# A hybrid decoder layer on one core: the transfers of sample states, requested by GpSimd in place of SyncE

## The chip, the cores and the metric

The kernel runs on one core of a Trainium2 chip. The metric is the time of one execution on the device in microseconds, the median of several runs. One execution is also recorded by the hardware profiler; a time inside it is counted from the start of its span. The engines are called by their names or as the profile has them: TensorE (PE, and PEld for its weight loads), VectorE (DVE), ScalarE (ACT), GpSimd (POOL), SyncE (SP, which here only requests transfers). Each engine works through its own queue in order; a waiting instruction holds up what is queued behind it on that engine.

## The reference, cut to what matters

One layer of a decoder runs over 16 learned tokens and 256 prompt tokens, and over one new token for each of 8 sequences (the samples), which start from states kept in memory:

```python
x = layer_norm(ALPHA * x + 0.5 * swiglu(x, f1_g, f1_u, f1_d), ...)
m, s_ret, s_hg = token_mixer(x, ...)
x = layer_norm(ALPHA * x + m, ...)
x = layer_norm(ALPHA * x + 0.5 * swiglu(x, f2_g, f2_u, f2_d), ...)

def token_mixer(x, pos, s_ret, s_hg, ...):
    q_r, k_r, v_r, g_r, q_h, f_h, i_h, g_h, a_r, a_h = split(x @ w_in, 10)
    ...
    s_ret, o_r = retention_chunk(s_ret, q_r, k_r, v_r)       # 8 heads, state 256 x 256
    s_hg, o_h = hgrn2_chunk(s_hg, q_h, k_h, i_h, log(f))     # 16 heads, state 128 x 128
    ...
    y = sigmoid(a_r) * o_r + sigmoid(a_h) * o_h
    return y @ w_out, s_ret, s_hg
```

For a sample both chunk functions have length 1. The new state is a decay times the old one plus the outer product of key and value; the output is the query times the new state. The decay is a constant of the head (retention) or a value for each feature (HGRN2). All new states are outputs. D_MODEL is 2048, the feed-forward width 5504, all data float32.

## The kernel before, in words

Features lie on the 128 partitions, the 280 tokens (272 and 8 samples) on the free axis. Every weight matrix is cut into 128x128 blocks and streamed once, 8 blocks (512 KB) to a unit. `stream` (L170) loads a unit into `raw` (L185, SyncE), ScalarE rounds it to `whi` (L188), and VectorE takes the rest, `wlo = raw - whi` (L189). `dense` (L204) multiplies each block in three matmuls, `xh·whi`, `xl·whi` and `xh·wlo` (L218). `raw`, `whi` and `wlo` have three buffers each.

The work runs as first feed-forward (`up`, `dn`), mixer, output projection (`wo`), second feed-forward. In the mixer the projections (`pj_...`) are streamed in 8 rounds, one for each retention head `u`, with two HGRN2 heads in each. The branches' own work is written as generators, `mix_hg` and `mix_ret`, which are started when their inputs are there and advanced a piece after each row of blocks (`pump`, L617). So their matmuls and vector work lie between those of the projections. TensorE's order is that of the code. The order on the other engines is made by a scheduler from the code and its own model of times.

What a round moves for the samples, by line:

- `mix_ret`, `load(e)` (L1092, transfers in L1095): the retention states of four samples, two tiles `smr` of 512 KB for each half `e`. Half 0 is loaded a round ahead; half 1 when the buffers of `ks` and `vs` are free, after the state matmuls (L1168).
- `spread(i)` (L1153, L1156): two samples' value rows, written to memory by L730 (`vrd`) and read back to all 128 partitions as `vbr` (256 KB, two buffers). `spread(0)` and `spread(1)` come early, `spread(2)` and `spread(3)` when the updates with the first two are done.
- L1192 (ScalarE) scales the old state by the decay, held in `gam` (L1174, GpSimd) for half 0 and in `late` (named `sro` in the profile, L1186 and L1188, GpSimd) for half 1. L1198 (VectorE) adds key times value, 16 updates a round; half 1 uses spreads 2 and 3.
- L1202: the four new tiles go out (`out_srs`), and L1211 multiplies them with the queries.
- `mix_hg`: the same for two HGRN2 heads: `load(h)` (L770, `smh`), `values(h)` (L774, `vbh`), `samples(h)` (L998 and L999), and out in L1002 (`out_sgs`). A one-element copy by GpSimd (L769, L773) stands ahead of each load to order it behind earlier work.

GpSimd also gathers `ends` (L750, L751), `tails` (L1103, transposed by TensorE in L1116) and `meta` (L910, L990). All transfers but two are requested by SyncE, so those of the states stand in one queue with the weights' loads.

Of the kernel before, what the change touches and what calls it, by code (L numbers as in the profile page):

```python
# [18 lines left out]
P = 128  # L19
# [109 lines left out]
def trunk(ctx: ExitStack, tc: tile.TileContext, A, O):  # L129
    nc = tc.nc  # L130
# [416 lines left out]
    with tc.tile_pool(name="yp", bufs=1) as yp:  # L547
# [7 lines left out]
        with tc.tile_pool(name="mp", bufs=1) as mp:  # L555
# [7 lines left out]
            def tmp(name, shape=(P, T), bufs=1, dt=F32, tag=None):  # L563
                if name in rows:
                    rows[name] = rows[name][1:] + rows[name][:1]
                    return rp.tile(list(shape), dt, tag=rows[name][-1], name=name)
                return mp.tile(list(shape), dt, tag=tag or name, name=name, bufs=bufs)
# [80 lines left out]
            def evacuate(n, c0, c1, o0, o1, b0, b1):  # L648
# [33 lines left out]
                elif n == "v_r":  # L682
                    v = tmp("v", (P, 2, T))
                    nc.scalar.copy(v[:, 0, :], o0)
                    nc.scalar.copy(v[:, 1, :], o1)
                    start(mix_ret(c0 // 2, st["q_r"], st["k_r"], v), 24 if c0 == 2 else 3)
                elif n in ("g_r", "g_h"):
                    sg = tmp("gs", (P, TL), bufs=2)
                    t = tmp("gt", (P, TL), bufs=2)
                    nc.scalar.activation(sg, o0, AF.Sigmoid)  # L690
                    mul(t, sg, o0)
                    sa = tmp("gs", (P, TL), bufs=2)
                    nc.scalar.activation(sa, o1, AF.Sigmoid)
                    mul(t, t, sa)
                    u, e = divmod(c0, 2)
                    while u not in (done_r if n == "g_r" else done_h):
                        pump()
                    if n == "g_r":
                        y = tmp("y", (P, TL))
                        mul(y, t, on_r[u][:, e, :])  # L700
                        st["y"] = y
                    else:
                        y = st["y"]
                        nc.vector.scalar_tensor_tensor(
                            out=t, in0=t, scalar=ngt[:, c0 : c0 + 1], in1=on_h[u][:, e, :], op0=ALU.mult, op1=ALU.mult)

                        ys[c0] = y if c0 < EARLY else yp.tile([P, TL], F32, tag=f"y{c0}", name=f"y{c0}")
                        add(ys[c0], y, t)
                        if c0 < EARLY:
                            split(yh[c0], yl[c0], y)  # L710
# [16 lines left out]
            def rows_out(src, width, tag):  # L727

                scr = drp.tile([NS, width], F32, tag=tag + "d", name=tag + "d")
                nc.sync.dma_start(scr, src)  # L730
                return scr
# [14 lines left out]
            def mix_hg(u, f, k, q, v):  # L746
# [16 lines left out]
                sms, vbs = [], []  # L763

                def load(h):

                    sms.append(tmp("smh", (P, NS, P), bufs=2))
                    vbs.append(tmp("vbh", (P, NS, P), bufs=2))
                    nc.gpsimd.tensor_copy(sms[h][:, 0, :1], kts[0][:, 0, :1] if h else acc[:, 15:16])  # L769
                    nc.sync.dma_start(sms[h], A["sg"][2 * u + h])  # L770

                def values(h):
                    nc.gpsimd.tensor_copy(vbs[h][:, 0, :1], kts[1][:, 0, :1] if h else acc[:, 2 * P + 15 : 2 * P + 16])  # L773
                    nc.sync.dma_start(vbs[h], vrow[h].partition_broadcast(P))  # L774


                Ts = {1: f}
# [92 lines left out]
                vrow = []  # L870
# [85 lines left out]
                if split_up:  # L956
                    load(0)
                    yield 4
                else:
                    for h in range(2):  # L960
                        if u:
                            fill(first(h), 1, h)
                        fill(second(h), 4, h)
                        if h == 0:
                            load(0)
                        yield 4
                for s in (16, 32, 64):
                    keep(tops[s], s)
                values(0)
                yield 15 if u == 1 else 2  # L970
                Tt = Ts[2 * LEVELS[-1]]
# [22 lines left out]
                def samples(h):  # L994
                    vb, sm = vbs[h], sms[h]
                    for b in range(NS):
                        at = NMETA + b
                        nc.scalar.activation(sm[:, b, :], sm[:, b, :], AF.Copy, scale=meta[:, h, at : at + 1])  # L998
                        nc.vector.scalar_tensor_tensor(  # L999
                            out=sm[:, b, :], in0=vb[:, b, :], scalar=meta[:, h, at + NS : at + NS + 1], in1=sm[:, b, :],  # L1000
                            op0=ALU.mult, op1=ALU.add)
                    nc.sync.dma_start(O["sgs"][2 * u + h], sm)  # L1002

                turned(0)
                load(1)
                yield 4
                turned(1)
                values(1)
                yield 7 if steady else 9
                gate()  # L1010
                samples(0)
                yield (6, 4, 4)[min(u, 2)]
                if u != 1:
                    samples(1)
                    yield 4 if u == 0 else 5
# [15 lines left out]
                if u == 1:  # L1031
                    yield 2
                    samples(1)
# [51 lines left out]
            def mix_ret(u, q, k, v):  # L1085
# [4 lines left out]
                sms = []  # L1090

                def load(e):  # L1092
                    for c in range(2):
                        sms.append(tmp("smr", (P, 4, 256), bufs=4))
                        nc.sync.dma_start(sms[2 * e + c], A["sr"][u, c, :, 4 * e : 4 * e + 4, :])  # L1095

                load(0)
                NB = BLOCKS[2][1]
                third = [slice(32 * i, 32 * i + NB) for i in range(3)]
# [35 lines left out]
                vrow = rows_out(vt2.rearrange("p c f -> p (c f)")[16:24, :], 256, "vr")  # L1135
# [15 lines left out]
                vbs = []  # L1151

                def spread(i):  # L1153
                    if i < 4:
                        vbs.append(tmp("vbr", (P, 2, 256), bufs=2))
                        nc.sync.dma_start(vbs[i], vrow[2 * i : 2 * i + 2, :].partition_broadcast(P))  # L1156

                spread(0)
                spread(1)
                yield 4  # L1160

                for c in range(2):
# [9 lines left out]
                    if c == 0:  # L1172
                        gams = [tmp("gam", (P, 1))]
                        nc.gpsimd.tensor_scalar(  # L1174
                            out=gams[0], in0=so[:, 0:1], scalar1=GAMMA[u], scalar2=GAMMA[u], op0=ALU.min, op1=ALU.max)
                    yield 2 if u or c == 0 else 10
                load(1)

                centre(vt.rearrange("p b c f -> p b (c f)"))
# [9 lines left out]
                for e in range(2):  # L1189
                    ss = sms[2 * e : 2 * e + 2]  # L1190
                    for sm in ss:
                        nc.scalar.activation(sm, sm, AF.Copy, scale=gams[e])  # L1192
                    for i in (2 * e, 2 * e + 1):
                        for c in range(2):
                            for b in (2 * i, 2 * i + 1):
                                x, t = ss[c][:, b - 4 * e, :], LP + b
                                kk = late_k[:, c, b - 4 : b - 3] if e else k[:, c, t : t + 1]
                                nc.vector.scalar_tensor_tensor(  # L1198
                                    out=x, in0=vbs[i][:, b - 2 * i, :], scalar=kk, in1=x, op0=ALU.mult, op1=ALU.add)
                        spread(i + 2)  # L1200
                    for c in range(2):
                        nc.sync.dma_start(O["srs"][u, c, :, 4 * e : 4 * e + 4, :], ss[c])  # L1202
                    yield 1 if e else 10 if u == 0 else 6
                yield (11 if u == 0 else 15) + 2 * calm
                pq = mx_bank("pqr")
# [171 lines left out]
```

## Time and profile before

| What | Value |
|---|---|
| Time, three runs | median 2566.4 us (2565.67 to 2569.12) |
| Span of the profiled execution | 2563.9 us; the page has no other time of this execution |
| Granted TensorE clock | 1.000 |
| TensorE busy | 2553.4 us |
| VectorE, ScalarE busy | 1702.8 us, 1392.2 us |
| GpSimd busy | 57.0 us, 152 instructions |
| Transfers | 536.26 MB, mean 209 GB/s |

The rows of the profile read as follows. A group or a timeline row names the line, the engine, the operation, `out<-in` by the program's names and the shapes. In a timeline the first two columns are start and duration in us, `xN` counts instructions that were merged, and a bracket at the end gives the idle time of the engine before it and what ended it. An SP row is the request alone, not the transfer. A row of waits has the total, the number and the longest, in us.

### The profile page before, as it was taken

The numbers are of one execution on the slowest core, as the hardware profiler recorded it, in microseconds if no ns is written. First come the engines' busy times: TensorE is split into PE (matmuls) and PEld (weight loads), VectorE is DVE, ScalarE is ACT, GpSimd is POOL, SyncE is SP. The second block draws the span as 40 slices with busy tenths as digits, with TensorE's granted clock in tenths as the row PEclk, the third lists the DMA queues.
The fourth block names the chain that finished last, engine by engine and source line by source line (L and its number), as shares of the span: only waits on it lengthen the run. The fifth ranks groups of instructions, "written<-read, shape, count | busy, mean of one in ns | idle before, by whom it ended". The sixth has DMA issues, their size and how long they took to land.

```text
span 2563.9 us, 56275 instructions
## 1 busy us (share of the span) xinstructions
PE 2553.4 (100%) x23424; PEld 2534.4 (99%) x23424; DVE 1702.8 (66%) x2827; ACT 1392.2 (54%) x2186; POOL 57.0 (2%) x152
## 2 busy tenths in 40 slices
PE   9999999999999999999999999999999999999999
PEld 9999999999999999999999999999999999999998
DVE  6444544475569878777777777777885555556555
ACT  5444444444456767767676666675564444444443
POOL 0000000000000000000000000000000000000000
PEclk9999999999999999999999999999999999999999
DMA  7555555555555876767676767675556565565554
GB/s 244 183 187 183 187 182 184 186 182 186 184 201 180 287 265 232 264 214 260 212 264 215 259 223 255 224 239 188 196 190 197 194 197 195 194 196 195 195 195 149
DMA packets 156897, 536.26 MB, mean 209 GB/s; under 512 B 17952, under 2 KB 25952, under 8 KB 156640
## 3 DMA queue, kind: packets, MB, share of 16 engines
q1 hardware_dynamic: 156352, 532.37, 62.0%
q8 instruction: 183, 3.00, 0.5%
q14 instruction: 74, 0.61, 0.1%
q10 hardware_dynamic: 288, 0.29, 0.0%
HBM read 501.99 MB, written 30.61 MB: 208 GB/s over the span
## 4 chain that ended last, share of the span: by engine, by line
PE 96%; DVE 2%; ACT 0%; issue 0%; DMA 0%; SPq 0%; ACTq 0%; DVEq 0%
PE up L218 36%; PE dn L218 19%; PE pj_i_h L218 3%; PE pj_g_r L218 3%; PE pj_q_h L218 3%; PE pj_g_h L218 3%; PE pj_a_r L218 3%; PE pj_a_h L218 3%; PE pj_f L218 3%; PE pj_q_r L218 3%; PE pj_k_r L218 3%; PE wo L218 3%; PE pj_v_r L218 3%; DVE wlo L189 1%; PE pqr L1211 1%; PE psr L1168 0%
## 5 line engine op out<-in xcount | busy, mean ns | idle before, releaser
L189 DVE TENSOR_TENSOR wlo<-raw,whi 128x1024 fp32r<-128x1024 f32 (+1 forms) x869 | 1062.2, 1223 | 740.7 <-ACT whi L188 737.3
L188 ACT CAST whi<-raw 128x1024 fp32r<-128x1024 f32 (+1 forms) x870 | 905.7, 1042 | 909.2 <-PE up L218 411.0
L218 PE MATMUL up<-xh,whi 128*128 128x280 f32 (+1 forms) x2624 | 725.6, 280 | 0.6 <-ACT whi L188 0.6
L218 PE MATMUL up<-xh,wlo 128*128 128x280 f32 (+1 forms) x2624 | 725.8, 280 | 0.4 <-DVE wlo L189 0.3
L218 PE MATMUL up<-xl,whi 128*128 128x280 f32 (+1 forms) x2624 | 725.4, 279 | 0.0
L218 PEld LDWEIGHTS up<-xh,wlo 128*128 128x128 f32 x2624 | 492.6, 189 | 1.0 <-DVE wlo L189 1.0
L218 PEld LDWEIGHTS up<-xh,whi 128*128 128x128 f32 x2624 | 492.6, 189 | 0.8 <-ACT whi L188 0.8
L218 PEld LDWEIGHTS up<-xl,whi 128*128 128x128 f32 x2624 | 492.6, 189 | 0.0
L218 PE MATMUL dn<-hh,whi 128*128 128x280 f32 (+1 forms) x1376 | 384.7, 280 | 0.0
L218 PE MATMUL dn<-hh,wlo 128*128 128x280 f32 (+1 forms) x1376 | 384.3, 279 | 0.0
L218 PE MATMUL dn<-hl,whi 128*128 128x280 f32 (+1 forms) x1376 | 384.3, 279 | 0.0
L218 PEld LDWEIGHTS dn<-hh,whi 128*128 128x128 f32 x1376 | 260.1, 189 | 0.1
L218 PEld LDWEIGHTS dn<-hl,whi 128*128 128x128 f32 x1376 | 260.1, 189 | 0.1
L218 PEld LDWEIGHTS dn<-hh,wlo 128*128 128x128 f32 x1376 | 260.1, 189 | 0.0
L218 PE MATMUL pj_k_r<-xh,whi 128*128 128x280 f32 x256 | 74.2, 290 | 0.0
L218 PE MATMUL pj_g_r<-xh,whi 128*128 128x264 f32 x256 | 74.0, 289 | 0.0
L218 PE MATMUL pj_v_r<-xh,whi 128*128 128x280 f32 x256 | 73.8, 288 | 0.0
L218 PE MATMUL pj_v_r<-xh,wlo 128*128 128x280 f32 x256 | 72.4, 283 | 0.3 <-DVE wlo L189 0.3
L218 PE MATMUL pj_g_h<-xh,whi 128*128 128x264 f32 x256 | 72.7, 284 | 0.0
L218 PE MATMUL pj_k_r<-xh,wlo 128*128 128x280 f32 x256 | 72.4, 283 | 0.0
L218 PE MATMUL pj_v_r<-xl,whi 128*128 128x280 f32 x256 | 72.3, 283 | 0.0
L218 PE MATMUL pj_k_r<-xl,whi 128*128 128x280 f32 x256 | 72.3, 283 | 0.0
(421 smaller groups left out, 5263.4 us busy)
## 6 DMA issues: line engine op xcount, KB each, us to landing
raw<-in_w_up SPq DMA_DIRECT2D x343, 512.0 KB, 4.1
raw<-in_w_in SPq DMA_DIRECT2D x320, 512.0 KB, 4.3
raw<-in_w_dn SPq DMA_DIRECT2D x172, 512.0 KB, 3.5
smr<-in_sr SPq DMA_DIRECT2D x32, 512.0 KB, 5.0
out_srs<-smr SPq DMA_DIRECT2D x32, 512.0 KB, 6.7
raw<-in_w_out SPq DMA_DIRECT2D x32, 512.0 KB, 3.9
vbr<-vrd SPq DMA_DIRECT2D x32, 256.0 KB, 4.1
smh<-in_sg SPq DMA_DIRECT2D x16, 512.0 KB, 5.2
```

The costliest lines, as they stand in the source:

```text
L188: nc.scalar.copy(hi[:, j:jn, :], raw[:, j:jn, :])
L189: nc.vector.tensor_tensor(out=lo[:, j0:j1, :], in0=raw[:, j0:j1, :], in1=hi[:, j0:j1, :].bitcast(F32), op=ALU.subtract)
L218: nc.tensor.matmul(o, w, t, start=start, stop=stop)
L1211: nc.tensor.matmul(pq[32 * j : 32 * j + 32, :256], qdr_at[c][:, 32 * b : 32 * b + 32], sms[2 * e + c][:, j, :], start=e + c == 0, stop=e + ...
```

## The change

Six calls of `nc.sync.dma_start` become `nc.gpsimd.dma_start`. Sizes, buffers and the one-element copies stay.

```diff
@@ mix_hg
                     nc.gpsimd.tensor_copy(sms[h][:, 0, :1], kts[0][:, 0, :1] if h else acc[:, 15:16])
-                    nc.sync.dma_start(sms[h], A["sg"][2 * u + h])
+                    nc.gpsimd.dma_start(sms[h], A["sg"][2 * u + h])
...
-                    nc.sync.dma_start(vbs[h], vrow[h].partition_broadcast(P))
+                    nc.gpsimd.dma_start(vbs[h], vrow[h].partition_broadcast(P))
...
-                    nc.sync.dma_start(O["sgs"][2 * u + h], sm)
+                    nc.gpsimd.dma_start(O["sgs"][2 * u + h], sm)
@@ mix_ret
-                        nc.sync.dma_start(sms[2 * e + c], A["sr"][u, c, :, 4 * e : 4 * e + 4, :])
+                        nc.gpsimd.dma_start(sms[2 * e + c], A["sr"][u, c, :, 4 * e : 4 * e + 4, :])
...
-                        nc.sync.dma_start(vbs[i], vrow[2 * i : 2 * i + 2, :].partition_broadcast(P))
+                        nc.gpsimd.dma_start(vbs[i], vrow[2 * i : 2 * i + 2, :].partition_broadcast(P))
...
-                        nc.sync.dma_start(O["srs"][u, c, :, 4 * e : 4 * e + 4, :], ss[c])
+                        nc.gpsimd.dma_start(O["srs"][u, c, :, 4 * e : 4 * e + 4, :], ss[c])
```

The other requests (`raw`, `dtab`, `vh0d`, `vh1d`, `vrd`, `out_srp`, `out_sgp`, `out_y`) stay with SyncE. TensorE's order is the same before and after; the other engines' orders move.

GpSimd's queue in round `u = 4`, from `tails<-v` to the copy of `meta` for the next round, before the change:

```order
L1103 COPY tails<-v 128x2x24 [waits Activation_49]
L1174 TENSOR_SCALAR gam<-sro 128x1 [waits Activation_49]
L1186 MEMSET sro 128x1 [waits DMAHW5_49,DMAHW4_49,Pool_49]
L1188 COPY sro<-k_r 128x8
L910 COPY meta<-K 128x2x16 [waits DVE_49,Activation_49]
```

The same place with the change, from the second `out_sgs` to the second `out_srs` (in the brackets DMASW is a transfer that GpSimd requested, DMAHW one of SyncE's):

```order
L1002 DMA out_sgs<-smh 128x1024 [waits DMASW7_49,DMASW4_49,DVE_49]
L1103 COPY tails<-v 128x2x24 [waits Activation_49]
L1156 DMA vbr<-vrd 128x512 [waits DMAHW7_49,DMASW0_49]
L1156 DMA vbr<-vrd 128x512 [waits DMASW1_49]
L1174 TENSOR_SCALAR gam<-sro 128x1 [waits Activation_49]
L1095 DMA smr<-in_sr 128x1024 [waits DMASW2_49,DVE_49,PE_49]
L1095 DMA smr<-in_sr 128x1024
L1186 MEMSET sro 128x1 [waits DMAHW4_49,DMAHW2_49,Pool_49]
L1188 COPY sro<-k_r 128x8
L1156 DMA vbr<-vrd 128x512 [waits DMASW0_49,DVE_49]
L1202 DMA out_srs<-smr 128x1024 [waits DMASW5_49,DVE_49,Activation_49]
L1156 DMA vbr<-vrd 128x512 [waits DMASW6_49,DMASW1_49,DVE_49]
```

`tails<-v` now has a request ahead of it, the two writes of `late` have the two loads of half 1 ahead of them, and the last spread stands behind an `out_srs`.

VectorE's queue in the same round, at its end, before (-) and with the change (+); 17004, 17046, 17076 and 17106 are four weight units in a row:

```order
 L1198 SCALAR_TENSOR_TENSOR smr<-vbr,k_r,smr 128x256 x2
 L189 TENSOR_TENSOR wlo_17004<-raw_17002,whi_17003 128x8x128
+L1198 SCALAR_TENSOR_TENSOR smr<-vbr,sro,smr 128x256 x3
 L189 TENSOR_TENSOR wlo_17046<-raw_17044,whi_17045 128x8x128
 L1198 SCALAR_TENSOR_TENSOR smr<-vbr,sro,smr 128x256 x5
 L189 TENSOR_TENSOR wlo_17076<-raw_17074,whi_17075 128x8x128
-L1198 SCALAR_TENSOR_TENSOR smr<-vbr,sro,smr 128x256 x3
 L240 TENSOR_TENSOR gt<-gs,pj_g_h_16864 128x264
 L189 TENSOR_TENSOR wlo_17106<-raw_17104,whi_17105 128x8x128
```

Three of the eight updates of half 1 moved from behind the split of unit 17076 to ahead of that of unit 17046, so all eight are now done before 17076 is split. The same piece stands in rounds 3 to 7.

## The prediction

> **What bounds the kernel now.** I read the page first: the span, the busy times and the chain that ended last.
>
> ```profile
> span 2563.9 us, 56275 instructions
> PE 2553.4 (100%) x23424; PEld 2534.4 (99%) x23424; DVE 1702.8 (66%) x2827; ACT 1392.2 (54%) x2186; POOL 57.0 (2%) x152
> PE 96%; DVE 2%; ACT 0%; issue 0%; DMA 0%; SPq 0%; ACTq 0%; DVEq 0%
> ```
>
> TensorE is the bound from end to end. The page shows no separate time for the profiled execution; its span is 2563.9 us, and the median of the three runs, 2566.4 us, lies 2.5 us above it. I add to the median what the change adds to the span. All the changed requests lie in the mixer, so the stretches of the mixer come next (windows: PE, PEld, DVE, ACT and POOL busy, the clock, the share of the 16 DMA engines, GB/s), with two pieces from the fifth of its eight rounds (u = 4).
>
> ```profile
> 827.00:1767.00 940.00, 939.80 (x9526) 925.58 (x9524) 742.40 (x1484) 637.33 (x1198) 50.80 (x124) 1.00 0.71 241
> ...
> 1303.00:1312.00 9.00, 9.00 (x82) 9.00 (x82) 7.33 (x13) 5.19 (x7) 0.00 (x0) 1.00 0.85 252
> 1312.00:1320.00 8.00, 8.00 (x114) 6.96 (x114) 6.51 (x12) 3.59 (x5) 0.00 (x0) 1.00 0.96 322
> ```
>
> TensorE is busy for 939.80 of 940.00 us. What it waited for is in the waits of TensorE (total, times, longest):
>
> ```profile
> PE pt L1116 <- POOL tails L1103: 0.9, 1, 0.9
> PE pj_f L218 <- DVE wlo L189: 0.7, 1, 0.7
> ...
> PE pj_v_r L218 <- DVE wlo L189: 0.3, 1, 0.3
> PE psc L1141 <- DVE acch L836: 0.2, 1, 0.2
> ```
>
> That is 2.1 us in the whole mixer, and a gain can hardly exceed it. 0.2% of the time is 5.1 us, about what a measurement of this kernel can tell from no change; so a gain that could be told from no change is nearly excluded, and the question is what new waits reach TensorE.
>
> **Where a wait would reach it.** TensorE reads its weights as `whi` (ScalarE) and `wlo` (VectorE), three buffers each. So I looked for the place where these are ready only just in time. It is at the end of each round. VectorE there (timeline, round u = 4), and the weight load that needs the split of 1310.97:
>
> ```profile
> 1304.12 0.88 DVE L1198 SCALAR_TENSOR_TENSOR smr<-vbr,k_r,smr 128x256 f32<-128x256 f32 x2
> 1304.91 1.22 DVE L189 TENSOR_TENSOR wlo<-raw,whi 128x1024 fp32r<-128x1024 f32 x1
> 1307.65 1.23 DVE L189 TENSOR_TENSOR wlo<-raw,whi 128x1024 fp32r<-128x1024 f32 x1 [1.52 <-ACT whi L188]
> 1308.79 2.26 DVE L1198 SCALAR_TENSOR_TENSOR smr<-vbr,sro,smr 128x256 f32<-128x256 f32 x5
> 1310.97 1.22 DVE L189 TENSOR_TENSOR wlo<-raw,whi 128x1024 fp32r<-128x1024 f32 x1
> 1312.10 1.27 DVE L1198 SCALAR_TENSOR_TENSOR smr<-vbr,sro,smr 128x256 f32<-128x256 f32 x3
> ...
> 1312.28 0.19 PEld L218 LDWEIGHTS pj_g_r<-xh,wlo 128*128 128x128 f32 x1
> ```
>
> The split ends at 1310.97 + 1.22 = 1312.19 and is read at 1312.28: 0.09 us to spare. What VectorE does just ahead of it depends on the state transfers that move.
>
> **The change, part by part.** *SyncE's side.* By the diff 18 requests a round leave its queue (four `smr`, four `vbr`, four `out_srs`, two each of `smh`, `vbh` and `out_sgs`), with the waits that belonged to them.
>
> ```profile
> 1298.07 0.40 SPq L1095 DMA_DIRECT2D smr<-in_sr  x1
> 1300.58 0.43 SPq L1095 DMA_DIRECT2D smr<-in_sr  x1
> ...
> 1303.36 1.99 SPq L1156 DMA_DIRECT2D vbr<-vrd  x2
> ...
> ACT whi L188 <- DMA raw<-in_w_in: 40.7, 27, 3.1
> ```
>
> Weights arrived late for ScalarE 27 times, 40.7 us in all, but the buffers covered that: TensorE's list has no row with `raw`. So this relief is worth 0 to 2.1 us; I take 1.0, half of the waits above, since two of the four rows are on `wlo`.
>
> *GpSimd's side: the price g of one request.* The trace has no request from GpSimd. The nearest rows:
>
> ```profile
> L1156 SPq DMA_DIRECT2D vbr<-vrd x32: 319/327/654, 824.7 to 1684.0; - x32
> ...
> L1103 POOL COPY tails<-k_r x8: 223/226/1638, 810.0 to 1653.7; 128x48 f32<-128x48 f32 x8
> L1103 POOL COPY tails<-v x8: 232/1112/1122, 819.0 to 1664.5; 128x48 f32<-128x48 f32 x8
> ```
>
> SyncE is held 0.33 us by the same request (minimum/median/maximum, ns); GpSimd's longest copy in these rows takes 1.64. I take g = 1.2 us, next to GpSimd's own usual row (1.11), since writing out 128 rows falls to the same engine; ends 0.33 and 1.64. For 18 requests a round that is 22 us of an engine with 2% to do: its sum costs nothing. What counts is who stands behind a request in GpSimd's queue.
>
> *The HGRN2 loads.* Four a round, and `meta` (L990), which ScalarE and VectorE need, now follows the last of them.
>
> ```profile
> 1262.06 0.33 SPq L770 DMA_DIRECT2D smh<-in_sg  x1
> 1271.04 0.42 SPq L774 DMA_DIRECT2D vbh<-vh1d  x1
> ...
> 1275.20 1.39 POOL L990 COPY meta<-fk 128x16 f32<-128x16 f32 x2 [0.28 <-PE ptm L988]
> 1280.37 1.92 DVE L999 SCALAR_TENSOR_TENSOR smh<-vbh,meta,smh 128x128 f32<-128x128 f32 x7
> ```
>
> The last request is possible at about 1270.7 and done by 1271.9, 3.3 us before `meta` is; the first state is asked for some 18 us before VectorE works on it, so a request or two of delay is covered. Cost 0. The writes (`out_srs`, `out_sgs`) are waited for by nothing until their buffers come round again.
>
> *Ahead of `tails`.* In rounds 2 to 7 `tails<-v` now stands behind the second `out_sgs`.
>
> ```profile
> 1283.36 0.87 DVE L999 SCALAR_TENSOR_TENSOR smh<-vbh,meta,smh 128x128 f32<-128x128 f32 x3
> 1285.31 1.22 DVE L189 TENSOR_TENSOR wlo<-raw,whi 128x1024 fp32r<-128x1024 f32 x1
> ...
> 1285.49 1.12 POOL L1103 COPY tails<-v 128x48 f32<-128x48 f32 x1 [8.90 <-ACT v L685]
> ...
> 1286.99 0.14 PEld L1116 LDWEIGHTS pt<-ident,tails 128*128 128x128 f32 x1
> ```
>
> That request becomes possible when VectorE ends its three updates, 1284.23, and ends at 1285.4 with g = 1.2; the copy began at 1285.49 anyway. It then ran to 1286.61, just past the end of VectorE's split (1286.53), where its free time is 0.23: it stood behind that split. So it may begin as late as about 1286.75 before TensorE waits at 1286.99, which is g up to 2.5. Cost 0 within my ends.
>
> *Ahead of `gam` and the second scale.* The two `smr` loads now follow `gam` on GpSimd, and the two small writes of `late` follow them.
>
> ```profile
> 1296.51 1.18 POOL L1174 TENSOR_SCALAR gam<-sro 128x1 f32<-128x1 f32 x1 [9.91 <-ACT sro L1170]
> 1298.77 0.19 POOL L1188 COPY sro<-k_r 128x8 f32<-128x8 f32 x1
> ...
> 1302.58 1.15 ACT L1192 ACTIVATE smr<-smr,sro 128x1024 f32<-128x1024 f32 x1 [0.20 <-DMA smr<-in_sr]
> 1305.53 1.15 ACT L1192 ACTIVATE smr<-smr,sro 128x1024 f32<-128x1024 f32 x1 [0.86 <-DMA smr<-in_sr]
> 1306.58 1.98 ACT L188 CAST whi<-raw 128x1024 fp32r<-128x1024 f32 x2
> ```
>
> From 1297.69 two requests take until 1300.1 and the writes until about 1300.4; ScalarE needs them at 1302.58, so 2.2 us are left. The second load is asked for at 1298.9 in place of 1300.58 and is whole at 1300.1, so it cannot well be later. Cost 0; the 0.86 us wait may shrink.
>
> *The spreading of the value rows.* This is the term that I count. The second one of the pair at L1156 may start when its buffer is free, after the two updates at 1304.12, thus at 1305.0. SyncE asked then (1303.36 + 1.99 less its own 0.33). GpSimd is free by about 1303 (1300.4, one spread and one `out_srs`), asks at 1305.0 too, and is done at 1306.2. From request to landing the rows say
>
> ```profile
> DMA to landing us min/median/max: 3.7/4.1/4.8
> ...
> out_srs<-smr SPq DMA_DIRECT2D x32, 512.0 KB, 6.7
> ```
>
> for these spreads (first row). Less SyncE's 0.33, 3.8 after the request is written: landing at 1310.0 (median before: 1309.1). VectorE's own order moves as well: in rounds 3 to 7 three of the eight later updates go ahead of the split of 1307.65 and five behind it, and of these five the second already needs this spread. With the first of the five done at 1309.2, VectorE stands until 1310.0; four updates (five took from 1308.79 to 1310.97, 0.44 each) take until 1311.75, the split until 1312.97. TensorE would wait 1312.97 − 1312.28 = 0.7 us. In general the wait is the landing less 1309.3. Five rounds: 3.5 us. Rounds 0 to 2 keep about their order, and there I count nothing. Ends: g = 0.33 and 3.8 give 1309.1, no wait; g = 1.64 and 4.5 (the row's 4.8 less 0.33) give 1311.1, so 1.8 us in five rounds, 9.0 us.
>
> The Trainium skill (DMA: Bandwidth & Descriptors, Anatomy of one DMA — SWDGE (gpsimd) path) prices such a transfer at about 2.0 us plus bytes / 436e3; 256 KB would then land an estimated 2.6 us after the start, at 1307.6, and the sum would be 2565.4. The rows above disagree: the same 256 KB took 4.1 us from SyncE, with the DMA engines 85% busy there.
>
> **Sum:** 2566.4 + 3.5 − 1.0 = 2568.9 us; on the span, 2563.9 + 2.5 = 2566.4. Ends of this case: 2566.4 − 2.1 = 2564.3 and 2566.4 + 9.0 = 2575.4.
>
> **The rivals.** *GpSimd's queue becomes late (slower).* If writing a request is held up by VectorE as `tails<-v` was (0.23 alone, 1.11 behind a split), g grows to 1.2 + 0.9 = 2.1. Five requests stand in a row from 1297.69 (two loads, spread, `out_srs`, spread) with 0.2 of small writes: the last ends at 1308.4 and not 1306.2, lands at 1312.2, and TensorE waits 2.9 us. In six rounds (2 to 7, where GpSimd's row is the same) 17 us: 2583 us. It decides from g = (1305.0 − 1297.9) / 4 = 1.8, where GpSimd is no longer free at 1305.0. For it: the slow copy is the usual one, 1.11 is the median of `tails<-v`. Against it: only 0.9 us of hold is seen, and a request is not a copy.
>
> The Trainium skill (SBUF — State Buffer, the practical consequences under its port table) says that a VectorE instruction with two SBUF inputs contends with a GpSimd instruction that reads SBUF, not with one that only writes it. The slow copy agrees for reading; no run here shows writing, and by that rule this rival would need another cause.
>
> *All hidden (no change).* If requests cost GpSimd about what they cost SyncE, the landing is at 1309.1, every stretch above has its margin, and only the relief is left: 2564.3 to 2566.4, say 2565.8 us. For it: TensorE's waits are 2.1 us now, and SyncE's queue gets shorter.
>
> *VectorE is held by GpSimd (slower).* Were each request to stop VectorE for its 1.2 us, the 18 would add 22 us to a round in which VectorE is 742.40 / 940.00 = 79% busy; between 1303 and 1312 it has 9.00 − 7.33 = 1.7 us free and about three requests to bear, 3.6 us, so 2 us a round and 16 in eight: 2582 us. Against it: the split of 1285.31, with GpSimd's copy beside it, takes 1.22 us like the others.
>
> **How the numbers follow.** Forecast (a small wait on the spread) 0.58; GpSimd late 0.20; hidden 0.17; VectorE held 0.05. Slower by over 0.2% is above 2571.5: the two slow rivals, 0.25, and the upper fifth of the forecast's own case (landing later than 1310.5, which is 1.2 us in five rounds less the 1.0), about 0.11, together 0.36. Faster by over 0.2% is below 2561.3, outside every sum here: 0.03 for what I have not seen. The same is left with 0.61. The range reaches from 2564.3 over the upper end of the forecast's case to the first slow rival, 2583; what lies beyond is under 2 in 10.
>
> **What would show it.** POOL's rows would give g: about 1.2 us, or 0.3, or 2. The landing row of the spread should read 4.6 to 5.4 from request to landing. VectorE should have a new wait `smr <- DMA vbr<-vrd` of about 0.8 us, five times, and TensorE a new row `pj_g_r <- DVE wlo` of about 3.5 us. If TensorE's waits stay at 2 us, hidden is right; if `gam`, `sro` or `tails` show up among the waits of ScalarE or TensorE, the queue is. A time under 2564 or over 2583 makes the prediction wrong.

## The result, and the profile after

The changed kernel takes 2584.45 us (median of four runs, 2581.78 to 2587.96) against 2567.76 us of the kernel before in the same set: a ratio of 1.0067, 95% interval 1.0053 to 1.0082. It is 17 us slower; the prediction said 2568.9, and not over 2583.0. The profiled execution of the changed kernel took 2587.96 us (span 2586.2), so it shows a little more loss than the median.

The head of its page, two queues and the engine shares of the chain:

```profile
span 2586.2 us, 56368 instructions
PE 2562.3 (99%) x23424; PEld 2539.3 (98%) x23424; DVE 1702.3 (66%) x2827; ACT 1391.3 (54%) x2186; POOL 135.9 (5%) x296
...
q1 hardware_dynamic: 135616, 465.26, 55.6%
q0 software_dynamic: 18688, 67.12, 7.5%
...
PE 89%; DVE 5%; DMA 3%; issue 1%; ACT 1%; POOL 0%; ACTq 0%; DVEq 0%; POOLq 0%
```

VectorE and ScalarE do the same work in the same time as before; TensorE's share of the chain fell from 96% to 89%, and DMA, at 0% before, has 3%. 67 MB now go through a second queue, q0. The mixer is the stretch from 829.3 to 1789.2 us, 959.9 us in place of 940.0:

```profile
829.30:1789.20 959.90, 947.59 (x9526) 930.21 (x9524) 741.95 (x1484) 636.57 (x1198) 127.44 (x264) 1.00 0.71 236
```

The granted clock is 1.00 on the average, as before. TensorE's waits in the mixer:

```profile
PE pj_g_h L218 <- DVE wlo L189: 3.8, 5, 0.8
PE pj_g_r L218 <- DVE wlo L189: 2.7, 3, 1.7
PE pj_g_h L218 <- ACT whi L188: 1.8, 2, 1.0
PE por L1226 <- DVE sc L255: 1.5, 1, 1.5
PE por L741 <- DVE osr L1083: 1.5, 1, 1.5
```

These rows add to 11.3 us; most of the rest of the 20 us sits in matmuls that last longer beside a wait (busy 947.59 against 939.80). A part of that is the clock. Behind two pairs of waits (1.53 and 1.47 us up to 966.4, 0.86 and 0.77 us up to 1577.8) it was granted at 0.50 for 3.4 us. Those two stretches, and then the same places in the kernel before:

```profile
967.10:970.50 3.40, 3.40 (x16) 3.22 (x16) 1.65 (x4) 2.00 (x5) 0.00 (x0) 0.50 1.07 371
1578.10:1581.50 3.40, 3.40 (x18) 3.40 (x18) 3.40 (x8) 1.44 (x2) 0.00 (x0) 0.50 0.89 255
```

```profile
958.80:962.20 3.40, 3.40 (x30) 3.35 (x29) 1.74 (x4) 2.51 (x6) 0.57 (x1) 1.00 1.03 383
1559.80:1563.20 3.40, 3.40 (x33) 3.40 (x32) 3.02 (x6) 1.68 (x3) 0.00 (x0) 1.00 0.82 187
```

TensorE is busy throughout all four, but gets through about half as many matmuls at 0.50. By half of 3.4 us, an estimate, each stretch costs 1.7 us on top of its waits. The waits for `por` (the retention outputs) are in round 1. The others in the list are for the weight halves of `pj_g_h` and `pj_g_r`, the last projections of a round. In round 4, ScalarE, VectorE, TensorE and the requests:

```profile
1311.18 1.09 POOL L1095 DMA_DIRECT2D smr<-in_sr  x2 [0.56 <-PE psr L1168]
...
1317.58 1.15 ACT L1192 ACTIVATE smr<-smr,sro 128x1024 f32<-128x1024 f32 x1 [2.25 <-DMA smr<-in_sr]
1318.63 1.03 ACT L188 CAST whi<-raw 128x1024 fp32r<-128x1024 f32 x1
...
1319.69 1.23 DVE L189 TENSOR_TENSOR wlo<-raw,whi 128x1024 fp32r<-128x1024 f32 x1 [1.77 <-ACT whi L188]
...
1320.97 0.38 PE L218 MATMUL pj_g_h<-xh,wlo 128*128 128x264 f32 x1 [0.77 <-DVE wlo L189]
```

Read it from the bottom: TensorE waits for a `wlo`, VectorE waits for its `whi`, ScalarE casts that `whi` only after it has stood 2.25 us at L1192 for a half-1 state. Before, the same wait was 0.20 us. The state loads of L1095, before and then after (duration of the request and landing, minimum/median/maximum):

```profile
L1095 SPq DMA_DIRECT2D smr<-in_sr x32: 328/432/1037, 745.2 to 1679.6; - x32
...
  ACT smr L1192: 7.4, 10
...
DMA to landing us min/median/max: 4.2/5.0/8.7
```

```profile
L1095 POOL DMA_DIRECT2D smr<-in_sr x32: 527/533/667, 747.6 to 1697.8; - x32
...
  ACT smr L1192: 16.2, 8
DMA to landing us min/median/max: 5.1/7.0/9.3
```

A request costs GpSimd 0.53 us, and its queue is not late; what got later is the landing. The two medians mix the halves: half 0, asked for a round ahead, landed after 6.9 to 8.7 us already in the kernel before (where its landing is on record), and after 5.7 to 9.3 now. For half 1 in rounds 3 to 7 it is 4.2 to 4.9 us before and 5.1 to 8.0 after. SyncE's own small transfers beside them suffer too. The landing row of `out_srp` (128 KB, from SyncE in both kernels) before, and after:

```profile
DMA to landing us min/median/max: 1.7/2.3/3.7
```

```profile
DMA to landing us min/median/max: 1.7/6.7/7.8
```

TensorE's order is the same in every kernel here, so the start of the same matmul can be compared between two traces. The `pj_g_h<-xh,wlo` above (1320.97) is this one of the kernel before:

```profile
1306.99 0.28 PE L218 MATMUL pj_g_h<-xh,wlo 128*128 128x264 f32 x1
```

By then 13.98 us were lost. Such differences, taken where a stretch ends, give the table below. A kernel that differed from the one before in nothing (below) showed 0.9 in the first column and 1.8 in the third, so differences of that size there are no finding.

| Profiled execution | to 827 us | round 0 (827–920) | round 1 (920–1000) | round 2 (1000–1100) | rounds 3–7 | median, us |
|---|---|---|---|---|---|---|
| after | 2.3 | 0.9 | 6.5 | 1.9 | 10.5 | 2584.5 |
| after_half1_sync | 0.9 | 1.4 | 5.7 | 1.5 | 15.3 | 2591.9 |
| before_half1_gpsimd | 0.2 | 0.0 | 4.1 | 1.2 | 19.4 | 2593.8 |
| before_spread_gpsimd | −0.3 | 1.4 | 4.4 | 1.6 | 20.1 | 2591.1 |
| before_writes_gpsimd | 0.7 | 0.3 | 5.7 | 2.1 | 5.1 | 2581.0 |
| before_hgrn2_gpsimd | 0.9 | 0.4 | 3.9 | 0.0 | 0.0 | 2569.0 |
| after_writes_sync | 1.6 | 1.7 | 4.4 | 3.0 | 10.7 | 2589.0 |
| before_vector_order | −0.1 | 0.0 | 0.7 | 0.0 | 5.5 | 2572.0 |
| before_spread_pinned | 1.2 | 1.4 | 5.1 | 1.7 | 5.9 | 2581.7 |
| before_half1_pinned | 0.3 | 0.0 | 5.0 | 3.8 | 7.5 | 2582.4 |
| before_writes_held | 0.7 | 0.3 | 5.3 | 0.0 | 0.6 | 2573.4 |
| before_spread_writes_held | 0.1 | 1.4 | 2.8 | 0.1 | 4.1 | 2575.7 |
| after_order_writes_held | 0.2 | 2.5 | 5.9 | 1.6 | 9.7 | 2585.6 |
| after_half1_sync_held | 1.4 | 1.4 | 5.3 | 0.0 | 4.2 | 2578.6 |
| before_half1_held | 0.9 | 0.0 | 1.6 | 1.0 | 7.6 | 2578.2 |
| before_half1_paced | 0.5 | 0.0 | 4.7 | 1.3 | 7.0 | 2577.7 |

The kernel before had medians of 2566.6 to 2567.8 us beside these.

### The profile page after: what moved, and what is told of

It is laid out like the page before. It is cut to its first block, busy times and chain, and to the rows that moved or that the text cites. A ratio compares the mean times of both kernels' runs of the same rounds, so it can differ in the third digit from the quotient of the medians.

```text
span 2586.2 us, 56368 instructions
## 1 busy us (share of the span) xinstructions
PE 2562.3 (99%) x23424; PEld 2539.3 (98%) x23424; DVE 1702.3 (66%) x2827; ACT 1391.3 (54%) x2186; POOL 135.9 (5%) x296
## 4 chain that ended last, share of the span: by engine, by line
PE 89%; DVE 5%; DMA 3%; issue 1%; ACT 1%; POOL 0%; ACTq 0%; DVEq 0%; POOLq 0%
PE up L218 35%; PE dn L218 18%; PE pj_q_r L218 3%; PE pj_k_r L218 3%; PE wo L218 3%; PE pj_f L218 3%; PE pj_i_h L218 3%; PE pj_v_r L218 3%; PE pj_q_h L218 3%; PE pj_g_r L218 3%; PE pj_a_r L218 3%; PE pj_g_h L218 2%; PE pj_a_h L218 2%; DVE wlo L189 2%; DMA smr<-in_sr 1%
## 5 line engine op out<-in xcount | busy, mean ns | idle before, releaser
L189 DVE TENSOR_TENSOR wlo<-raw,whi 128x1024 fp32r<-128x1024 f32 (+1 forms) x869 | 1062.3, 1223 | 760.5 <-ACT whi L188 757.9
L218 PE MATMUL pj_g_h<-xh,wlo 128*128 128x264 f32 x256 | 71.8, 280 | 3.8 <-DVE wlo L189 3.8
L218 PE MATMUL pj_g_r<-xh,wlo 128*128 128x264 f32 x256 | 71.2, 278 | 2.7 <-DVE wlo L189 2.7
```

What stands on the lines that cost most here:

```text
L189: nc.vector.tensor_tensor(out=lo[:, j0:j1, :], in0=raw[:, j0:j1, :], in1=hi[:, j0:j1, :].bitcast(F32), op=ALU.subtract)
L218: nc.tensor.matmul(o, w, t, start=start, stop=stop)
```

## The experiments

### One part at a time

The first theory (A) was the chain read above: half-1 loads late, so ScalarE, so the weights. Its rivals were the writes (W) and the prediction's own term, the spreads (S). The first kernel is the changed one with half 1 given back to SyncE:

```diff
-                        nc.gpsimd.dma_start(sms[2 * e + c], A["sr"]...
+                        (nc.sync if e else nc.gpsimd).dma_start(sms[2 * e + c], A["sr"]...
```

> The changed kernel with one call taken back: the two retention-state loads of half 1 (L1095 with e = 1) are requested by SyncE again; half 0, spreads, writes and all HGRN2 transfers stay with GpSimd. Theory A (the half-1 loads, asked for as a pair by GpSimd, land 2 to 3 us later, ScalarE stands at L1192 in front of the next weight cast, and the late whi and wlo stop TensorE once a round): nearly all of the 17 us goes, 2567 to 2571 us, and the idle time ahead of L1192 falls from 16.2 us to about 8. Theory W (the writes out_srs and out_sgs, on a queue of their own, take the DMA engines from the weights): 2580 to 2585. Theory S (the prediction's term, the spreads): 2580 to 2585.

Measured: 2591.93 us, ratio 1.0098 (1.0085 to 1.0112). Not a recovery, but 7 us worse than the full change. ScalarE's wait for `smr` was back to 8.2 us as expected, and something else had taken its place: VectorE's wait for `vbr` went from 6.0 us to 17.4. The second is the reverse, on the kernel before:

```diff
-                        nc.sync.dma_start(sms[2 * e + c], A["sr"]...
+                        (nc.gpsimd if e else nc.sync).dma_start(sms[2 * e + c], A["sr"]...
```

> The kernel before with one call moved: only the two half-1 loads of L1095 are requested by GpSimd. Theory A: most of the loss appears, 2577 to 2585 us, with landings of 6 to 8 us for these loads where SyncE's took 4.5 to 5. Theories W and S: 2566 to 2569, no change.

Measured: 2593.8 us, 1.0106 (1.0092 to 1.0119): half of one call costs 27 us, more than all six calls. Next, only the spreads:

```diff
-                        nc.sync.dma_start(vbs[i], vrow[2 * i : 2 * i + 2, :]...
+                        nc.gpsimd.dma_start(vbs[i], vrow[2 * i : 2 * i + 2, :]...
```

> The kernel before with only the spreads (L1156) requested by GpSimd. Theory S, as the prediction had it: 2570 to 2577 us, with a wait of VectorE on vbr and of TensorE on wlo. Theories A and W: 2566 to 2569. VectorE's order moves here too, as it does in the full change (three half-1 updates ahead of the split); if that order alone did the harm, this kernel would show it as well.

Measured: 2591.13 us, 1.0095 (1.0081 to 1.0108), far beyond S. Its VectorE in round 4:

```profile
1315.46 0.87 DVE L1198 SCALAR_TENSOR_TENSOR smr<-vbr,k_r,smr 128x256 f32<-128x256 f32 x2
1318.80 0.88 DVE L1198 SCALAR_TENSOR_TENSOR smr<-vbr,sro,smr 128x256 f32<-128x256 f32 x2 [2.47 <-DMA vbr<-vrd]
1319.59 1.22 DVE L189 TENSOR_TENSOR wlo<-raw,whi 128x1024 fp32r<-128x1024 f32 x1
```

In the kernel before, a split (1304.91) follows the two `k_r` updates at once. Here the scheduler has put two half-1 updates ahead of that split, VectorE stands 2.47 us in front of them, and the weight split waits behind. So a moved order is a cause of its own. Only the writes (L1202, L1002):

```diff
-                    nc.sync.dma_start(O["sgs"][2 * u + h], sm)
+                    nc.gpsimd.dma_start(O["sgs"][2 * u + h], sm)
...
-                        nc.sync.dma_start(O["srs"][u, c, :, 4 * e : 4 * e + 4, :], ss[c])
+                        nc.gpsimd.dma_start(O["srs"][u, c, :, 4 * e : 4 * e + 4, :], ss[c])
```

> The kernel before with only the writes (out_srs, L1202, and out_sgs, L1002) requested by GpSimd; the order of ScalarE, VectorE and TensorE is that of before, instruction for instruction. Theory W: 2575 to 2585 us, the weights land later beside the writes. Theories A and S: 2564 to 2568, no change or a small gain, since SyncE's queue loses the waits in front of the writes.

Measured: 2581.03 us, 1.0055 (1.0042 to 1.0069), with no order moved on TensorE, VectorE and ScalarE. Three single parts thus cost 14 to 27 us each, and everything together 17: the parts do not add up, and A, W and S as first put all fell. (The half-0 loads were not tried alone.) The cheap part is HGRN2:

```diff
-                    nc.sync.dma_start(sms[h], A["sg"][2 * u + h])
+                    nc.gpsimd.dma_start(sms[h], A["sg"][2 * u + h])
...
-                    nc.sync.dma_start(vbs[h], vrow[h].partition_broadcast(P))
+                    nc.gpsimd.dma_start(vbs[h], vrow[h].partition_broadcast(P))
...
-                    nc.sync.dma_start(O["sgs"][2 * u + h], sm)
+                    nc.gpsimd.dma_start(O["sgs"][2 * u + h], sm)
```

> The kernel before with only the HGRN2 transfers (smh, vbh, out_sgs: L770, L774, L1002) requested by GpSimd; the order of TensorE, VectorE and ScalarE is that of before. The prediction put these at 0: 2566 to 2568 us. If a second queue costs round 1 about 5 us whatever it carries (round 1 lost 4 to 5 us in nearly every kernel, its DMA engines being busy throughout): 2570 to 2573. If these transfers delay the weights in every round as the retention states do: 2575 to 2582.

Measured: 2568.99 us, 1.0007 (0.9998 to 1.0016): no difference that this can tell, and 0.0 us in rounds 2 to 7 (3.9 in round 1, in an execution 2 us above the median). So a second queue is not dear whatever it carries. The last of this group is the changed kernel with its writes back on SyncE (the diff of the writes, reversed):

> The changed kernel with the writes out_srs and out_sgs back on SyncE; the order of ScalarE, VectorE and TensorE is that of the changed kernel, instruction for instruction. The writes alone cost 14 us on the kernel before. If parts add up, this is 2570 to 2572. If the loads are enough for the round-end waits (theory A), 2576 to 2582, with the stall of round 1 (about 5 us, late weights) gone. If the reads were all of it: 2584.

Measured: 2589.02 us, 1.0090 (1.0075 to 1.0106). The reads alone are enough for the loss, and taking the writes back does not help.

### The order by itself

Order edges hold VectorE's half-1 updates of rounds 3 to 7 either as before or as after; `los` lists the weight splits, `ups` a round's eight half-1 updates, `n` the number of splits so far, True means that the split goes first, and an edge of the kind ORDER adds no wait between engines:

```diff
+        first, then = (los[n], inst) if split_first else (inst, los[n])
+        tc.add_manual_dep(then, first.name, kind)
...
+# as before
+    return [(n + 2, x, True, ORDER) for x in ups] + [(n + 3, x, True, ORDER) for x in ups[5:]] + [(n + 3, x, False, ORDER) for x in ups[:5]]
+# as after
+    return [(n + 2, x, False, ORDER) for x in ups[:3]] + [(n + 2, x, True, ORDER) for x in ups[3:]] + [(n + 3, x, False, ORDER) for x in ups]
```

First the order of the changed kernel alone, all transfers from SyncE:

> The kernel before, all transfers from SyncE, with VectorE's order of the changed kernel in rounds 3 to 7 (three half-1 updates ahead of the split of unit 17046, the other five ahead of that of 17076), set by order edges alone; the second out_srs of half 0 follows the first on SyncE, nothing else moves. Theory O (a moved order puts a wait for a state transfer ahead of a weight split): the first spread of half 1 lands at about 1307.4 of round 4, three updates end at 1308.7, the split of 17046 at 1309.9, five updates at 1312.1, the split of 17076 at 1313.3 where TensorE reads at 1312.3: about 1 us a round, 2571 to 2574 us. Theory A (half-1 loads requested by GpSimd land late): no change, 2566 to 2568.

Measured: 2571.95 us, 1.0019 (1.0010 to 1.0028), 5.5 us in rounds 3 to 7. Shown, at the size expected. TensorE's and VectorE's new waits:

```profile
PE pj_g_r L218 <- DVE wlo L189: 1.6, 4, 0.6
...
DVE smr L1198 <- DMA vbr<-vrd: 6.8, 6, 1.4
```

Then spreads and half-1 loads alone, with VectorE's order held to that of before:

> The spreads alone requested by GpSimd, as in before_spread_gpsimd, but VectorE's order of rounds 3 to 7 held to that of before. Theory O: the loss of before_spread_gpsimd (24 us, most of it a wait of 2.5 us a round for vbr ahead of a split) was the order, 2567 to 2572 us. If the loss came from GpSimd's spreads landing late whatever stands behind them: 2580 to 2590. The prediction's own term was 3.5 us in five rounds.

Measured: 2581.72 us, 1.0058 (1.0045 to 1.0071).

> The half-1 loads alone requested by GpSimd, as in before_half1_gpsimd, with VectorE's order of rounds 3 to 7 held to that of before. Theory A: the pair lands 6 to 8 us after the request, ScalarE waits for it at L1192 ahead of a weight cast, and about 1.5 us a round is left: 2575 to 2581 us. Theory O: the loss goes, 2567 to 2571.

Measured: 2582.36 us, 1.0059 (1.0046 to 1.0071). The order was 9 us of the spreads' 24 and 11 us of the loads' 27. Part of that is the clock: in before_spread_gpsimd it was 0.50 for 13.6 us (from 1190.6, 1450.0 and 1709.5 us), with the order held for 3.4 us (from 947.4). By half of the difference, an estimate, that is 5 of the 9 us, a consequence of the longer waits. Some 15 us are left in each kernel, again as much as the writes cost.

> A second look at before_spread_pinned, unchanged, on the chip of the three other kernels of this set, as the reference for the next one: 2579 to 2585 us.

Measured: 2582.86 us in one run.

### The time of the writes

The requests gave the next theory, T: the writes cost time because they are asked for sooner. With the writes on GpSimd, round 4 reads:

```profile
1312.20 0.57 POOL L1202 DMA_DIRECT2D out_srs<-smr  x1 [3.67 <-ACT vs L718]
1315.37 0.53 POOL L1202 DMA_DIRECT2D out_srs<-smr  x1 [2.59 <-DVE smr L1198]
...
1312.81 0.33 SPq L185 DMA_DIRECT2D raw<-in_w_in  x1
1313.19 1.97 SPq L1156 DMA_DIRECT2D vbr<-vrd  x2
1315.97 0.33 SPq L185 DMA_DIRECT2D raw<-in_w_in  x1
```

The same place in the kernel before:

```profile
1302.99 0.33 SPq L185 DMA_DIRECT2D raw<-in_w_in  x1
...
1306.16 0.33 SPq L185 DMA_DIRECT2D raw<-in_w_in  x1
1306.54 0.42 SPq L1202 DMA_DIRECT2D out_srs<-smr  x1
```

There the two spreads went in between (1303.36, the row in the prediction), and SyncE's queue asked for the first write, 512 KB that nothing waits for, 3.2 us after the first spread, behind a weight load that waits for a split. On GpSimd the write goes 1 us ahead of the spread (1312.20 against 1313.19). SyncE's queue was a priority list by accident. Taking the spreads out of it frees the writes in the same way; in before_spread_pinned:

```profile
1313.76 0.33 SPq L185 DMA_DIRECT2D raw<-in_w_in  x1
1314.14 0.43 SPq L1202 DMA_DIRECT2D out_srs<-smr  x1
```

The write follows the first weight load 0.4 us later, where it was 3.6 us. So each `out_srs` was held until the weight split that it follows in the kernel before, by a dependence (WAIT) on that split:

```diff
-                    for c in range(2):
-                        nc.gpsimd.dma_start(O["srs"][u, c, ...], ss[c])
+                    for c, n in zip(range(2), {0: (1, 3, 2, 3), 1: (1, 3, 3, 4)}.get(u, (2, 3, 4, 5))[2 * e :]):
+                        links.append((len(los) + n, nc.gpsimd.dma_start(O["srs"][u, c, ...], ss[c]).ins, True, WAIT))
```

> The writes alone requested by GpSimd, as in before_writes_gpsimd, but each out_srs held until the weight split that it follows in the kernel before (there SyncE's queue had put it behind the load of a weight unit, which waits for that split; in rounds 2 to 7 it is the split of unit 17004, 17046, 17106 and the next one, in the names of round 4). Theory T (the loss comes from writes that are asked for 2 to 4 us sooner and then share the DMA engines with the spread and the weights): 2566 to 2570 us. Theory R (a second queue beside SyncE's costs this by itself, whenever it asks): 2578 to 2583.

Measured: 2573.35 us, 1.0025 (1.0015 to 1.0035). In rounds 2 to 7 the loss fell from 7.2 us to 0.6 (table): there theory T is shown, and a second queue by itself cost these transfers nothing. VectorE's wait for the spreads, first with the writes early, then held:

```profile
DVE smr L1198 <- DMA vbr<-vrd: 12.4, 9, 2.5
```

```profile
DVE smr L1198 <- DMA vbr<-vrd: 4.2, 4, 2.4
```

What is left is round 1, 5.3 us. The same hold in before_spread_pinned, where SyncE asks for the writes:

> The spreads alone requested by GpSimd, VectorE's order held, and the writes, which SyncE still requests, each held until the weight split that it follows in the kernel before. Without the spreads in SyncE's queue its first out_srs was asked for about 3.5 us sooner, ahead of the last spread. Theory T: 2566 to 2571 us. Theory R: 2578 to 2583, since the spreads still come from a second queue.

Measured: 2575.73 us, 1.0037 (1.0024 to 1.0049), between the two theories: 6 us of the 15 were the early writes. In rounds 3 to 7, 4.1 us are left to the spreads themselves. Last, the full change with both:

> The full change, all six transfers from GpSimd, with VectorE's order of rounds 3 to 7 held to that of before and each out_srs held until the weight split that it follows in the kernel before. If order (5 us) and early writes are all of the loss: 2567 to 2572 us. Theory A (the pair of half-1 loads, asked for back to back by GpSimd, is late by itself): 2574 to 2580, with ScalarE's wait at L1192 still near 16 us. Theory R: 2580 or more.

Measured: 2585.57 us, 1.0074 (1.0060 to 1.0088). Holding order and writes does not help the full change; there theory A is back, with ScalarE's wait as long as ever:

```profile
ACT smr L1192 <- DMA smr<-in_sr: 18.4, 9, 3.1
```

### The half-1 loads

With order and writes out of the way, the loads could be tried again. The first kernel below is the full change so held, with half 1 on SyncE:

> The full change with VectorE's order and the out_srs held as in after_order_writes_held, and the half-1 loads back on SyncE. Theory A (in the full change these loads are what the round's end waits for): 2573 to 2579 us, the spread's 4 us in rounds 3 to 7 and the loss of rounds 0 to 2 being left. If the half-1 loads matter no more than the other five calls: 2582 to 2587.

Measured: 2578.55 us, 1.0045 (1.0032 to 1.0057): 7.0 us less than the same kernel with half 1 on GpSimd. With order and writes held, these loads are thus the largest part of the full change that was measured. In after_half1_sync the same step had not helped: there order and writes were free, and VectorE's wait for `vbr` was 17.4 us. Which of the two hid the gain was not tried. The two rows of state loads in after_half1_sync_held, half 0 from GpSimd and half 1 from SyncE (the last figure is the median landing in us):

```profile
smr<-in_sr POOLq DMA_DIRECT2D x16, 512.0 KB, 9.1
...
smr<-in_sr SPq DMA_DIRECT2D x16, 512.0 KB, 4.9
```

Half 0 is asked for a round ahead and may be late (SyncE's row for it in before_half1_held has 8.0 us, so the 9.1 is not mainly GpSimd's doing); half 1 is back at SyncE's usual landing, and ScalarE's wait halves:

```profile
ACT smr L1192 <- DMA smr<-in_sr: 8.9, 12, 1.7
```

Then the loads alone on the kernel before, so held, and with GpSimd's second request set back:

> The half-1 loads alone requested by GpSimd, VectorE's order and the out_srs held. Theory A: the loads are late by themselves, 2574 to 2581 us, ScalarE's wait at L1192 near 16 us. Theory T (early writes beside them made them late): 2567 to 2571, that wait near 8 us.

Measured: 2578.15 us, 1.0045 (1.0032 to 1.0059).

```diff
+                        e and c and tc.add_manual_dep(ld.ins, copies[1].name, WAIT)
```

> As before_half1_held, but GpSimd's second half-1 load is held until ScalarE's second copy of sro, which is what SyncE's queue had ahead of it in the kernel before (there the two loads were 2.5 us apart, here 0.55). Pair theory (two loads of 512 KB asked for together delay each other): 2567 to 2572 us, landings near 5 us. Ring theory (a load that GpSimd requests lands later beside SyncE's transfers, whatever its distance from the next): as before_half1_held, 2574 to 2581, landings of 6 us and more.

Measured: 2577.65 us, 1.0043 (1.0030 to 1.0055), the same: setting the second load back gains nothing. It does not clear the pair, though. In rounds 3 to 7 the first load landed after 5.0 to 5.7 us, where it took 5.5 to 7.4 with the second close behind; but the second, asked for about 2.1 us after the first, still took 6.3 to 7.3 us, and ScalarE's wait for the loads went from 15.7 to 19.2 us. The row of half 1 in the page of the held kernel, then of the paced one:

```profile
smr<-in_sr POOLq DMA_DIRECT2D x16, 512.0 KB, 6.7
```

```profile
smr<-in_sr POOLq DMA_DIRECT2D x16, 512.0 KB, 6.4
```

### The transfer by itself

> A measurement by itself, away from the mixer: in the kernel before, every fourth weight unit of the feed-forwards' up matrices (512 KB) is requested by GpSimd, which has nothing else to do there; SyncE's took 3.5 to 4.1 us to land. If GpSimd's transfers are slow by themselves: 5.5 to 7 us. If only the company in the mixer makes them late: 4 to 5 us, about SyncE's plus a longer start. Time within 5 us of 2567 in the second case.

Measured: 2568.5 us in one run. The condition matched no matrix, so this was the kernel before once more, and serves only as the gauge of the table. With the right condition (`N_UP` is 172):

```diff
-                    nc.sync.dma_start(raw[:, j0:j1, :], src[:, j0:j1, :])
+                    (nc.gpsimd if n_units == N_UP and u % 4 == 3 else nc.sync).dma_start(raw[:, j0:j1, :], src[:, j0:j1, :])
```

> The measurement that before_up_quarter was meant to make (its condition matched no weight matrix, so it was the kernel before once more): every fourth weight unit (512 KB) of the feed-forwards' matrices of 172 units is requested by GpSimd, which has nothing else to do there; SyncE's took 3.5 to 4.1 us to land. If GpSimd's transfers are slow by themselves: 5.5 to 7 us. If only the company in the mixer makes them late: 4 to 5 us. In the second case the time stays within 5 us of 2567.

Measured: 2566.86 us, 0.9998 (0.9989 to 1.0008), and the landings:

```profile
raw<-in_w_up SPq DMA_DIRECT2D x257, 512.0 KB, 3.8
...
raw<-in_w_up POOLq DMA_DIRECT2D x86, 512.0 KB, 3.7
```

GpSimd's 512 KB are not slow by themselves, 3.7 us against 3.8. The half-1 loads are late only in the mixer's company, 6.7 us where SyncE's take 4.9. Not every load is late there: in before_hgrn2_gpsimd GpSimd's 512 KB of `smh` land after 5.9 us, against 4.8 to 6.2 from SyncE in three kernels, and those of `vbh` after 5.8 against 6.6. How the DMA engines share out their time there was not tried. The Trainium skill (DMA: Bandwidth & Descriptors, Queues, rings and completion order) says that each DMA engine goes round-robin between the queue rows that have work, a packet at a time. That agrees with SyncE's `out_srp` landing after 6.7 us in place of 2.3 beside GpSimd's loads; no run here shows the turns.

## Why the prediction was wrong, point by point

- **The bound and the sensitive place** were right for rounds 3 to 7: TensorE lost 10.5 us there, at the ends of rounds, on late weight halves. The margin of 0.09 us fits that so many different edits cost about the same there and do not add up: the latest one counts, and hides the rest.
- **Rounds 0 to 2** were put at nothing in the spreads' term, because they "keep about their order", and no other term adds anything there. By the table they cost 9.3 us of the 22 in the profiled execution, 6.5 of them in round 1. Some 5 us of these lie around 965 us, where TensorE waits twice for `por` and the halved clock follows.
- **GpSimd's price g** was put at 1.2 us (0.33 to 1.64); it is 0.53. ScalarE's wait for `gam` (9.2 us in seven times) and TensorE's for `tails` (0.9, once) are the same before and after, so the rival of a late GpSimd queue was wrong, and its 2583 us fell near the result by another cause. VectorE was not held either: 1702.3 us busy against 1702.8. The Trainium skill's rule that the prediction cited (SBUF — State Buffer, the practical consequences under its port table) agrees: 1223 ns is the mean of a weight split in both kernels.
- **The step that failed** is "Ahead of `gam` and the second scale": the second load "cannot well be later. Cost 0". The request was in time, as worked out; the landing was not. The step took the landing to be as far behind the request as SyncE's was. Half 1 lands 6.7 us after GpSimd's request where SyncE's takes 4.9, ScalarE stands up to 3.4 us in front of a weight cast, and giving these loads back is worth 7.0 us (2585.57 to 2578.55). In round 4 it was the first of the two loads that ScalarE stood for, whose landing the step did not price at all (6.3 us after its request at 1311.18).
- **The spreads**, forecast at 3.5 us in five rounds, cost 4.1 there with order and writes held, and 4.2 in after_half1_sync_held. The wait is the one forecast (`pj_g_r <- DVE wlo`, 3.0 us in four times in before_spread_writes_held), but that the size came out is partly luck: the request took 0.54 us and not 1.2, the last spread landed 5.4 to 6.5 us after its start and not 5.0 (1.2 + 3.8), and VectorE's order was held where the forecast had counted on the moved one. In the full change the term is mostly covered by the later half-1 loads (VectorE's wait for `vbr` is 6.0 us in four times there).
- **VectorE's order** was read and then priced only through a late spread. Alone, with every transfer in SyncE's time, it costs 5 us (2571.95). In the full change it is covered: holding it, and the writes, gained nothing.
- **The writes**, "waited for by nothing", were put at 0. They cost 14 us alone; 7.7 of these came back when they were held, so that much is due to their being asked for sooner. In the full change taking them back to SyncE gained nothing (2589.02 against 2584.45).
- **SyncE's relief**, −1.0, did not come: ScalarE's wait for weights went from 40.7 us to 46.6. It could hardly have come, since the waits it was taken from lie ahead of nearly all the moved requests: TensorE is idle 2.1 us from 746 to 827 us, and 0.2 from 827 to 1767. A queue with fewer waits asks for everything sooner, the things that can wait as well.
- **The HGRN2 loads** at 0 were right to within some 4 us (1.0007, 0.9998 to 1.0016).

What stays open: 11.9 us remain in after_half1_sync_held. 4.2 of them are in rounds 3 to 7, with the spreads. Round 1 has 5.3 in that execution and 4 to 6 in most kernels with state transfers on GpSimd, of which up to 1.8 is there in the kernel before repeated. In after_half1_sync_held most of it is one wait of TensorE for `wlo` (2.6 us at 947.4), behind VectorE's 2.8 us wait for `vbr`, and a clock of 0.50 for 3.4 us right after it; but other kernels lose theirs elsewhere in the round, and the cause was not settled. In the full change and with half 1 on GpSimd, a state scaling of round 1 (L1192) also goes ahead of a weight cast on ScalarE; that order was not held in any kernel. Why a GpSimd load lands later beside SyncE's stays open too. No kernel here beat the one before.

## What to carry to other kernels

A transfer queue is a schedule: before moving part of it to another engine, ask what stood behind each moved request and will now be asked for sooner, and hold what can wait behind what cannot. Price the landing in the company that it will have, not the request, since 512 KB from GpSimd took 3.7 us in the feed-forward and 6.7 for half 1 in the mixer. Where the path has no margin, parts tried one at a time neither add up nor clear each other; hold the instruction order and the request times, then take the parts back one by one.

## What the runs showed of the hardware

- A request of states, spreads or writes costs GpSimd 0.53 to 0.54 us (medians), against SyncE's 0.33 to 0.43 for the retention states and spreads.
- In the feed-forward, away from the state traffic, a 512 KB load lands as fast from GpSimd as from SyncE (3.7 and 3.8 us); for the half-1 loads in the mixer it takes about 1.8 us longer (6.7 against 4.9).
- Beside GpSimd's loads, SyncE's 128 KB writes took 6.7 us to land in place of 2.3 (6.3 in before_half1_held, 4.1 with GpSimd's two loads set apart): the queue that did not change pays too.
- A wait of TensorE can cost more than itself. Behind waits of 1.53 and 1.47 us, and of 0.86 and 0.77, the granted clock was 0.50 for 3.4 us; behind 0.96 and 0.77 (1706.8 and 1708.1 us) it stayed at 1.00. What decides it was not tried.
